# Gate and up products of two feed-forward layers by blocks with seven products in place of eight

## The chip, the cores and the metric

The kernel runs on one core of a Trainium2 chip. Its engines are TensorE (PE in the profile, PEld its weight loads), VectorE (DVE), ScalarE (ACT), GpSimd (POOL) and SyncE (SP, which issues most of the transfers); each works through its own instructions in order and waits for the others by semaphores. The metric is the device time of one execution in microseconds, smaller is better. Before the change it was 1977.13 us, the median of 3 runs (1977.07 to 1987.16).

## The reference

Two transformer blocks follow each other on 512 tokens of width 1024, in float32. Both end with a gated feed-forward layer of width 2816, and only these two layers change:

```python
hffn = modulate(rmsnorm(x, g_norm2[l]), shift2, scale2)
a, u = jnp.split(jnp.einsum('bsd,df->bsf', hffn, w_ffn_in[l]), 2, axis=-1)
x = x + gate2[:, None, :] * jnp.einsum('bsf,fd->bsd', jax.nn.silu(a) * u, w_ffn_out[l])
...
h = rmsnorm_2(x, norm_ffn[l])
x = x + (jax.nn.silu(h @ w_ffn_gate[l]) * (h @ w_ffn_up[l])) @ w_ffn_down[l]
```

The rest (modulation, stick-breaking attention and retention in the first block, sparse attention and gated linear attention in the second) is as before.

## The kernel before

Activations lie transposed: a tile holds 128 channels and all 512 tokens. Every float32 operand is split into a high part in the reduced format float32r (ACT, `split` and `weights`, L150 and L172) and the rest as a low part (DVE, L151 and L173). A product of two such operands is three matmuls, high-high, high-low and low-high (`mm3`, L160 to L162). PSUM has banks under four names: g (3), z (2), r (2) and o (1).

`gemm` (L179) makes 256 output columns: per step it takes four tiles of 128 weight rows, 512 KB, which SP loads into a raw tile (L169), splits them into wh and wl, and runs 24 matmuls of 512 columns into two banks; eight weight tiles are two steps, 48 matmuls. There are three raw, wh and wl tiles each. `gemm_halves` (L213) does the same in two halves of 256 tokens, so that the first half can start when half of its input is normed.

`joint` adds an output projection to the residual and norms the result in halves (`fin2`, `fin4`). `ffn_hidden` then walks over 11 pairs of a gate gemm and an up gemm of 256 columns (the first gate gemm in halves): the gate's bank goes through a sigmoid on ACT and a product on DVE (L869, L870), the up's bank is multiplied in on DVE (L873), and the hidden tile is split at once into two p or q tiles (L150, L151). The output projection over 22 hidden tiles follows.

The order on each engine is written by the framework's scheduler from the order of the program and from what is ready by its own estimate; a tile of a name that has no free buffer waits for one to be released. SBUF holds 32 tiles named p and 36 named q of 2 KB per partition, 12 named t, and the raw, wh and wl tiles of 4 KB.

Of the kernel before, what the change touches and what calls it, by code (L numbers as in the profile page):

```python
# [9 lines left out]
F32 = mybir.dt.float32  # L10
# [57 lines left out]
SLOTS = {"p": 32, "q": 36, "t": 12, "k": 3, "raw": 3, "wh": 3, "wl": 3}  # L68
# [7 lines left out]
N_DIRECT = 2  # L76

# [44 lines left out]
def build(tc, A, dump=None):  # L122
    nc = tc.nc
    with ExitStack() as es:
# [3 lines left out]

        def new(tag, dt=F32):
            return P.tile([128, T], dt, tag=tag, name=tag, bufs=SLOTS[tag])  # L130

# [4 lines left out]
        def wtile(tag, shape, dt):  # L136
            return P.tile(shape, dt, tag=tag, name=tag, bufs=SLOTS[tag])

# [74 lines left out]
        def gemm_halves(w, kt, c0, ncol, X, evac, mid=None, n0=0):  # L213
# [4 lines left out]
            for hf in range(2):  # L218
# [11 lines left out]
                if mid is not None:  # L230
                    mid(hf)

# [535 lines left out]
        def ev_merge(n, ps):  # L768
# [79 lines left out]
        H2 = [pair("p") for _ in range(KD)]  # L848

        def fin2(hf, st):  # L850
            rc = small("rc", 16, bufs=2)
            rstd(st, 0, rc, 0)
            R = psum("r")
            spread(R, rc, 0, 2)
            for k in range(KD):
                norm_mod(x2[k], R[:, 0:256], a2[:, k:k + 1], mod[:, 24 + k:25 + k], H2[k], HS[hf])
# [3 lines left out]
        def ffn_hidden(w_a, ca, w_u, cu, X):  # L860
            hid = []
            for c in range(11):
                act = {}

                def ev_a(n, ps, sl=slice(0, T)):
                    s = new("t")
                    if n not in act:
                        act[n] = new("t")
                    nc.scalar.activation(s[:, sl], ps, AF.Sigmoid)  # L869
                    nc.vector.tensor_mul(act[n][:, sl], ps, s[:, sl])  # L870
# [12 lines left out]
        hid = ffn_hidden(A["w_ffn_in"], 0, A["w_ffn_in"], FF, H2)  # L883


# [526 lines left out]
```

## Time and profile before

| | |
|---|---|
| median of the runs | 1977.13 us |
| the profiled execution | 1982.96 us |
| its span, first to last instruction | 1981.2 us |
| mean granted clock of TensorE | 0.976 |
| PE, DVE, ACT, POOL busy | 96%, 54%, 37%, 16% |
| loads of the first layer's gate and up weights | 851.2 to 1093.7 us |
| loads of the second layer's gate and up weights | 1535.7 to 1813.8 us |

The busy shares are of the span of one profiled execution. A matmul's shown duration includes the time until its results are through, in which the next one already runs; what counts is the distance between starts. A group of instructions shows the busy time, the mean of one and the idle time of its engine just before, with what ended it.

### The profile page before, as it was taken

The page shows a single profiled execution, that of the slowest core. Times are in us where ns is not written, and L with a number is a line of the kernel's source. Part 1 is how long each engine was busy: PE and PEld are TensorE (multiplying, and loading weights), DVE is VectorE, ACT ScalarE, POOL GpSimd, SP SyncE. Part 2 cuts the span into 40 slices and gives each one's busy share as a digit, 9 for nine tenths or more (in the row PEclk, how much of TensorE's full clock was granted, in tenths as well). Part 3 has the DMA queues.
Part 4 walks back from the last instruction along what each step waited for, and adds up shares of the span by engine and source line. Part 5 has one row for each costly group of instructions (what it writes and reads, how often), then busy time and mean ns, then how long its engine had stood idle before and what let it go on. Part 6 is the DMA issues. An engine that isn't in the chain of part 4 may idle for free. (4 is left out here: it accounts for less than half of the span.)

```text
span 1981.2 us, 24637 instructions
## 1 busy us (share of the span) xinstructions
PE 1897.3 (96%) x9561; PEld 1575.5 (80%) x9561; DVE 1074.8 (54%) x1754; ACT 729.4 (37%) x1250; POOL 315.0 (16%) x357
## 2 busy tenths in 40 slices
PE   6889999999999999999999999979999999999998
PEld 4678777888879898888888888767877788888886
DVE  6888876645464554663443322587377653443222
ACT  3466654233322323343222222552255532222222
POOL 3232211102030302010000012232343300000000
PEclk7999999999999999999999999989899999999999
DMA  6612222433424244523332233232133123333222
GB/s 210 203 54 65 65 64 86 159 123 107 133 90 139 77 137 124 195 77 105 96 93 90 89 112 114 79 102 64 31 93 101 49 70 96 96 96 89 92 85 75
DMA packets 193521, 199.25 MB, mean 101 GB/s; under 512 B 9718, under 2 KB 178692, under 8 KB 193404
## 3 DMA queue, kind: packets, MB, share of 16 engines
q1 hardware_dynamic: 189920, 188.48, 30.9%
q0 software_dynamic: 3136, 9.08, 1.4%
q8 instruction: 75, 1.23, 0.3%
q14 instruction: 42, 0.34, 0.1%
q10 hardware_dynamic: 348, 0.13, 0.0%
HBM read 189.25 MB, written 9.99 MB: 101 GB/s over the span
## 5 line engine op out<-in xcount | busy, mean ns | idle before, releaser
L160 PE MATMUL ps_g<-p,wh 128*128 128x512 f32 (+1 forms) x1464 | 579.7, 399 | 8.5 <-DVE q L475 2.6
L161 PE MATMUL ps_g<-p,wh 128*128 128x512 f32 (+1 forms) x1464 | 576.6, 394 | 2.8 <-DVE p L405 2.8
L162 PE MATMUL ps_g<-p,wl 128*128 128x512 f32 (+1 forms) x1464 | 575.9, 394 | 0.0
L173 DVE TENSOR_TENSOR wl<-raw,wh 128x1024 fp32r<-128x1024 f32 (+1 forms) x262 | 325.3, 1242 | 448.9 <-ACT wh L172 448.0
L172 ACT CAST wh<-raw 128x1024 fp32r<-128x1024 f32 (+1 forms) x282 | 294.4, 1044 | 651.7 <-PE ps_g L161 378.9
L160 PEld LDWEIGHTS ps_g<-p,wh 128*128 128x128 f32 x1464 | 276.5, 190 | 74.0 <-issue 7.7
L161 PEld LDWEIGHTS ps_g<-p,wh 128*128 128x128 f32 x1464 | 277.5, 190 | 63.5 <-DVE p L405 3.6
L162 PEld LDWEIGHTS ps_g<-p,wl 128*128 128x128 f32 x1464 | 277.1, 189 | 62.6
L203 PE MATMUL ps_g<-wh,p 128*128 128x256 f32 x512 | 149.1, 292 | 1.5 <-ACT wh L172 1.5
L204 PE MATMUL ps_g<-wl,p 128*128 128x256 f32 x512 | 146.4, 286 | 1.2 <-DVE wl L173 1.2
L205 PE MATMUL ps_g<-wh,p 128*128 128x256 f32 x512 | 146.6, 286 | 0.0
L160 PE MATMUL ps_g<-q,wh 128*128 128x512 f32 (+1 forms) x368 | 142.4, 390 | 0.1
L161 PE MATMUL ps_g<-q,wh 128*128 128x512 f32 (+1 forms) x368 | 142.1, 386 | 0.0
L162 PE MATMUL ps_g<-q,wl 128*128 128x512 f32 (+1 forms) x368 | 142.0, 386 | 0.0
L203 PEld LDWEIGHTS ps_g<-wh,p 128*128 128x128 f32 x512 | 99.6, 195 | 2.8 <-ACT wh L172 1.9
L204 PEld LDWEIGHTS ps_g<-wl,p 128*128 128x128 f32 x512 | 99.8, 195 | 1.9 <-DVE wl L173 1.4
L205 PEld LDWEIGHTS ps_g<-wh,p 128*128 128x128 f32 x512 | 99.7, 195 | 0.0
L160 PEld LDWEIGHTS ps_g<-q,wh 128*128 128x128 f32 x368 | 69.5, 189 | 15.5 <-DVE p L790 0.3
L162 PEld LDWEIGHTS ps_g<-q,wl 128*128 128x128 f32 x368 | 69.5, 189 | 15.0
L161 PEld LDWEIGHTS ps_g<-q,wh 128*128 128x128 f32 x368 | 69.5, 189 | 14.6
L150 ACT CAST q<-t 128x512 fp32r<-128x512 f32 (+1 forms) x68 | 39.1, 581 | 87.2 <-DVE t L873 48.8
L319 DVE SCALAR_TENSOR_TENSOR adaacc<-raw,cact,adaacc 128x256 f32<-128x256 f32 x112 | 53.9, 481 | 27.2 <-DMA raw<-in_w_ada 25.4
(373 smaller groups left out, 2619.4 us busy)
## 6 DMA issues: line engine op xcount, KB each, us to landing
raw<-in_w_in SPq DMA_DIRECT2D x108, 512.0 KB, 3.6
raw<-in_w_ffn_in SPq DMA_DIRECT2D x44, 512.0 KB, 3.5
raw<-in_w_ada SPq DMA_DIRECT2D x32, 512.0 KB, 3.4
raw<-in_w_ffn_gate SPq DMA_DIRECT2D x22, 512.0 KB, 3.6
raw<-in_w_ffn_up SPq DMA_DIRECT2D x22, 512.0 KB
raw<-in_w_ffn_down SPq DMA_DIRECT2D x22, 512.0 KB, 3.7
raw<-in_w_ffn_out SPq DMA_DIRECT2D x19, 512.0 KB, 3.4
raw<-in_w_proj_ret SPq DMA_DIRECT2D x16, 512.0 KB, 3.3
```

What stands on the lines that cost most here:

```text
L150: nc.scalar.copy(hi, src)
L160: nc.tensor.matmul(ps, lh, rh, start=start, stop=False)
L161: nc.tensor.matmul(ps, lh, rl, start=False, stop=False)
L162: nc.tensor.matmul(ps, ll, rh, start=False, stop=stop)
L172: nc.scalar.copy(wh, raw)
L173: low_engine["e"].tensor_tensor(out=wl, in0=raw, in1=f(wh), op=ALU.subtract)
L203: nc.tensor.matmul(o, xh[:, ts], wh[:, i], start=k == 0 and t % 2 == 0, stop=False)
L204: nc.tensor.matmul(o, xh[:, ts], wl[:, i], start=False, stop=False)
L205: nc.tensor.matmul(o, xl[:, ts], wh[:, i], start=False, stop=k == KD - 1 and t % 2 == 1)
L319: nc.vector.scalar_tensor_tensor(out=acc, in0=w, scalar=c, in1=acc, op0=ALU.mult, op1=ALU.add)
```

## The change

For nine of the eleven pairs of a layer, gate and up columns are computed together as a product of two by two blocks. X is cut into halves of tokens (i) and of channels (j), X11 to X22; the weights into halves of channels (i) and into gate (j = 1) and up (j = 2). Seven products, each of 256 tokens, 512 channels and 256 columns (24 matmuls of 256 columns), with weight sums T and activation sums S, take the place of eight:

- 1: X11 with W11; 2: X12 with W21;
- 6: T6 = W11 + W12 + W22; 7: T7 = W12 + W22; 5: T5 = W11 + W12; 3: W22; 4: T4 = W11 + W12 + W21 + W22.

The sums of X are made once per layer (`Normed.sums`) on DVE; signs are chosen so that all weight combinations are sums, and the up results come out negated, which the last product undoes. Products 1, 6, 5 and 3 accumulate in one bank, copied out in between by ACT; 2 has its own; 7 and 4 share a third (`Block.after`).

The weight sums are transfers from SBUF to SBUF that add to their destination, issued by POOL (`Block.add`): raw(1,2) into raw(1,1), which is T5; T5 into a second load of W22 (T6); raw(2,2) into raw(1,2) (T7); T6 into raw(2,1) (T4). A block has five loads of 512 KB, one of them that second load, and four adds of 512 KB. `woven` sets the order 1 2 6 7 5, then 1 of the next block, 3, 4, 2 of the next block, and so on; `play` prepares two products ahead.

The first two pairs of a layer stay plain, in halves (`gemm_quarters`), while the sums of X are formed. All hidden tiles stay whole in 22 p tiles and are split at the end. The memory of q, raw, wh and wl becomes a region that is laid out for the mixing part or for the blocks (16 S tiles of 4 KB, 5 raw) and changes four times; a tile of the new layout waits for the tiles whose memory it takes. The merged activations go to p tiles instead of q.

```diff
 NVEC = _o
-SLOTS = {"p": 32, "q": 36, "t": 12, "k": 3, "raw": 3, "wh": 3, "wl": 3}
+SLOTS = {"p": 32, "t": 12, "k": 3}
+MIX = {"q": 36, "raw": 3, "wh": 3, "wl": 3}
+FFN = {"S": 16, "raw": 5, "wh": 3, "wl": 3}
...
+        region = {}
+        def lay_out(slots):
+            if region:
+                region.pop("es").close()
+            region["es"] = ExitStack()
+            region["pool"] = region["es"].enter_context(tc.tile_pool(name="rg", bufs=1, reuse_waits="tile"))
+            region["slots"] = slots
+        es.callback(lambda: region.pop("es").close())
         def new(tag, dt=F32):
-            return P.tile([128, T], dt, tag=tag, name=tag, bufs=SLOTS[tag])
+            if tag in SLOTS:
+                return P.tile([128, T], dt, tag=tag, name=tag, bufs=SLOTS[tag])
+            return region["pool"].tile([128, T], dt, tag=tag, name=tag, bufs=region["slots"][tag])
...
         def wtile(tag, shape, dt):
-            return P.tile(shape, dt, tag=tag, name=tag, bufs=SLOTS[tag])
+            return region["pool"].tile(shape, dt, tag=tag, name=tag, bufs=region["slots"][tag])
...
+        def gemm_quarters(w, c0, X, evac, n0=0):
+            ws = [weights(w, b, 4, c0, 256) for b in (0, 4)]
+            for hf in range(2):
+                ps = psum("gz"[hf])
+                for n in range(2):
+                    s = slice(n * 128, n * 128 + 128)
+                    for k in range(KD):
+                        wh, wl = ws[k // 4]
+                        xh, xl = X.at(k, hf)
+                        o = ps[:, n * 256:n * 256 + 256]
+                        st, sp = n == 0 and k == 0, n == 1 and k == KD - 1
+                        nc.tensor.matmul(o, wh[:, k % 4, s], xh, start=st, stop=False, skip_group_check=True)
+                        nc.tensor.matmul(o, wh[:, k % 4, s], xl, start=False, stop=False, skip_group_check=True)
+                        nc.tensor.matmul(o, wl[:, k % 4, s], xh, start=False, stop=sp, skip_group_check=True)
+                for n in range(2):
+                    evac(n0 + n, hf, ps[:, n * 256:n * 256 + 256])
+        lay_out(MIX)
...
-            merged[n] = split_new(P2[n], "q")
+            merged[n] = split_new(P2[n], "p")
...
+        lay_out(FFN)
...
-        H2 = [pair("p") for _ in range(KD)]
+        class Normed:
...
+            def quarter(self, i, j):
+                if (i, j) not in self.Q:
+                    self.Q[i, j] = [wtile("S", [128, 4, 256], F32R) for _ in range(2)]
+                return self.Q[i, j]
...
+            def sums(self):
+                def of(i, j, k):
+                    return self.X[4 * (j - 1) + k][:, HS[i - 1]]
+                t = {n: [new("t") for _ in range(2)] for n in (6, 7)}
+                tt = {n: [x.rearrange("p (k n) -> p k n", n=256) for x in t[n]] for n in t}
+                for k in range(4):
+                    a, b, c, d = of(1, 1, k), of(1, 2, k), of(2, 1, k), of(2, 2, k)
+                    s2, s3 = tt[6][k // 2][:, k % 2], tt[7][k // 2][:, k % 2]
+                    nc.vector.tensor_sub(s3, a, c)
+                    nc.vector.tensor_sub(c, d, c)
+                    nc.vector.scalar_tensor_tensor(out=s2, in0=c, scalar=-1.0, in1=a, op0=ALU.mult, op1=ALU.subtract)
+                    nc.vector.scalar_tensor_tensor(out=a, in0=b, scalar=-1.0, in1=s2, op0=ALU.mult, op1=ALU.subtract)
+                    yield
+                for n in (6, 7, 5, 3):
+                    self.S[n] = [wtile("S", [128, 4, 256], F32R) for _ in range(2)]
+                    hi, lo = self.S[n]
+                    if n in t:
+                        for h in range(2):
+                            split(tt[n][h], hi[:, 2 * h:2 * h + 2], lo[:, 2 * h:2 * h + 2])
+                    else:
+                        for k in range(4):
+                            split(of(2 if n == 5 else 1, 1, k), hi[:, k], lo[:, k])
+                    yield
+                self.S[1], self.S[2], self.S[4] = self.Q[1, 1], self.Q[1, 2], self.Q[2, 2]
+                del self.Q[2, 1]
...
+            def add(self, out, a):
+                nc.gpsimd.dma_start(out, a, accum_op=ALU.add)
+            def prep(self, i):
+                raw = self.raw
+                if i == 1:
+                    self.load(1, 1)
+                    src = raw[1, 1]
+                elif i == 2:
+                    self.load(2, 1)
+                    src = raw[2, 1]
+                elif i == 6:
+                    self.load(1, 2)
+                    self.load(2, 2)
+                    t5, t7, t4 = raw[1, 1], raw[1, 2], raw[2, 1]
+                    self.add(t5, raw[1, 2])
+                    t6 = wtile("S", [128, self.kn, 256], F32)
+                    self.load(2, 2, t6)
+                    self.add(t6, t5)
+                    self.add(t7, raw[2, 2])
+                    self.add(t4, t6)
+                    self.T = {6: t6, 7: t7, 5: t5, 3: raw[2, 2], 4: t4}
+                    src = t6
+                else:
+                    src = self.T[i]
+                wh = wtile("wh", [128, self.kn, 256], F32R)
+                wl = wtile("wl", [128, self.kn, 256], F32R)
+                split(src, wh, wl)
+                self.w[i] = wh, wl
+            BANK = {1: "A", 6: "A", 5: "A", 3: "A", 2: "B", 7: "C", 4: "C"}
+            TAG = {"A": "g", "B": "z", "C": "r"}
+            def product(self, i):
+                b = self.BANK[i]
+                first, last = i in (1, 2, 7), i in (3, 2, 4)
+                if first:
+                    self.ps[b] = psum(self.TAG[b])
+                ps = self.ps[b]
+                wh, wl = self.w.pop(i)
+                sh, sl = self.X.S[i]
+                for n in range(2):
+                    o = ps[:, n * 256:n * 256 + 256]
+                    s = slice(n * 128, n * 128 + 128)
+                    for k in range(self.kn):
+                        st = first and n == 0 and k == 0
+                        sp = last and n == 1 and k == self.kn - 1
...
+                            nc.tensor.matmul(o, wh[:, k, s], sh[:, k], start=st, stop=False, skip_group_check=True)
+                            nc.tensor.matmul(o, wh[:, k, s], sl[:, k], start=False, stop=False, skip_group_check=True)
+                            nc.tensor.matmul(o, wl[:, k, s], sh[:, k], start=False, stop=sp, skip_group_check=True)
...
+            def after(self, i):
+                if i in (1, 6, 5):
+                    self.sb[i] = new("t")
+                    nc.scalar.copy(self.sb[i], self.ps["A"])
+                if i == 2:
+                    nc.vector.tensor_add(self.sb[1], self.ps["B"], self.sb[1])
+                    self.out(1, 1, self.sb[1])
+                if i in (5, 7) and {5, 7} <= self.done:
+                    nc.vector.tensor_add(self.sb[5], self.ps["C"], self.sb[5])
+                    self.out(2, 2, self.sb[5])
+                if i == 3:
+                    self.out(1, 2, self.ps["A"])
+                if i == 4:
+                    nc.vector.tensor_add(self.sb[6], self.ps["C"], self.sb[6])
+                    self.out(2, 1, self.sb[6])
+        def play(steps):
+            for b, i in steps[:2]:
+                b.prep(i)
+            for n, (b, i) in enumerate(steps):
+                if n + 2 < len(steps):
+                    c, j = steps[n + 2]
+                    c.prep(j)
+                b.product(i)
+                yield b, i
+        def woven(blocks):
+            steps = []
+            for n, b in enumerate(blocks):
+                if n == 0:
+                    steps += [(b, 1), (b, 2)]
+                steps += [(b, 6), (b, 7), (b, 5)]
+                if n + 1 < len(blocks):
+                    c = blocks[n + 1]
+                    steps += [(c, 1), (b, 3), (b, 4), (c, 2)]
+                else:
+                    steps += [(b, 3), (b, 4)]
+            return steps
...
-        def ffn_hidden(w_a, ca, w_u, cu, X):
...
-                def ev_u(n, ps):
-                    nc.vector.tensor_mul(act[n], ps, act[n])
-                    i = len(hid)
-                    hid.append(split_new(act[n], "p" if i < 4 else "q"))
-                if c == 0:
-                    gemm_halves(w_a, KD, ca, 256, X, lambda n, hf, ps: ev_a(n, ps, HS[hf]))
-                else:
-                    run(gemm(w_a, KD, ca + 256 * c, X, ev_a))
-                run(gemm(w_u, KD, cu + 256 * c, X, ev_u))
-            return hid
+        def ffn_hidden(wa, ca, wu, cu, X):
+            hid = [new("p") for _ in range(2 * N_PLAIN)]
+            sums = X.sums()
+            act = {}
...
+            for c in range(N_PLAIN):
+                gemm_quarters(wa, ca + 256 * c, X, ev_a, n0=2 * c)
+                gemm_quarters(wu, cu + 256 * c, X, ev_u, n0=2 * c)
+                for _ in range(4):
+                    next(sums, None)
+            run(sums)
+            blocks = []
+            for s in range(N_PLAIN, 11):
+                hold = {}
+                hid += [new("p") for _ in range(2)]
+                def out(i, j, c, s=s, hold=hold):
+                    if j == 1:
+                        g = new("t")
+                        nc.scalar.activation(g, c, AF.Sigmoid)
+                        (nc.vector if i == 1 else nc.gpsimd).tensor_tensor(out=c, in0=c, in1=g, op=ALU.mult)
+                    hold[i, j] = c
+                    if (i, 1) in hold and (i, 2) in hold:
+                        for e in range(2):
+                            es = slice(e * 256, e * 256 + 256)
+                            nc.vector.scalar_tensor_tensor(out=hid[2 * s + e][:, HS[i - 1]], in0=hold[i, 2][:, es], scalar=-1.0,
+                                                           in1=hold[i, 1][:, es], op0=ALU.mult, op1=ALU.mult)
+                blocks.append(Block((range(0, 4), range(4, 8)), ((wa, ca + 256 * s), (wu, cu + 256 * s)), X, out))
+            for _ in play(woven(blocks)):
+                pass
+            lay_out(MIX)
+            return [split_new(h, "q" if 2 <= i < 20 else "p") for i, h in enumerate(hid)]
```

## Rows read from the trace of the kernel before

**Rows 1.** The page: span, engines' busy time, granted clock in 40 slices.

```profile
span 1981.2 us, 24637 instructions
...
PE 1897.3 (96%) x9561; PEld 1575.5 (80%) x9561; DVE 1074.8 (54%) x1754; ACT 729.4 (37%) x1250; POOL 315.0 (16%) x357
...
PEclk7999999999999999999999999989899999999999
```

**Rows 2.** Windows: length, busy us by engine, clock, DMA share, GB/s.

```profile
906.00:1096.00 190.00, 190.00 (x816) 153.05 (x816) 74.71 (x84) 54.68 (x68) 0.00 (x0) 1.00 0.31 94
...
1614.00:1819.00 205.00, 205.00 (x880) 165.07 (x879) 80.80 (x91) 58.94 (x73) 0.00 (x0) 1.00 0.33 95
```

**Rows 3.** Timeline of PE, 512 columns (start, us): first and last of 80.

```profile
1085.24 0.40 PE L161 MATMUL ps_g<-p,wh 128*128 128x512 f32 x1
...
1103.68 0.40 PE L162 MATMUL ps_g<-p,wl 128*128 128x512 f32 x1
```

**Rows 4.** Timeline of PE, 256 columns: first and last of 48.

```profile
862.03 0.28 PE L160 MATMUL ps_g<-q,wh 128*128 128x256 f32 x1
...
867.60 0.27 PE L162 MATMUL ps_g<-q,wl 128*128 128x256 f32 x1
```

**Rows 5.** Groups by line, 906 to 1096 us: busy us, mean ns, idle before.

```profile
L173 DVE TENSOR_TENSOR wl<-raw,wh 128x1024 fp32r<-128x1024 f32 x34 | 41.7, 1226 | 86.8 <-ACT wh L172 86.8
L172 ACT CAST wh<-raw 128x1024 fp32r<-128x1024 f32 x34 | 35.8, 1052 | 96.6 <-PE ps_g L161 60.3 <-issue 36.3
...
L873 DVE TENSOR_TENSOR t<-ps_g,t 128x512 f32<-128x512 f32 x16 | 11.1, 691 | 11.6 <-PE ps_g L162 11.6
L869 ACT ACTIVATE t<-ps_g 128x512 f32<-128x512 f32 x18 | 10.7, 594 | 17.4 <-PE ps_g L162 17.4
...
L150 ACT CAST q<-t 128x512 fp32r<-128x512 f32 x14 | 8.6, 617 | 19.0 <-DVE t L873 19.0
```

**Rows 6.** Timeline of DVE, operations on 256 columns.

```profile
875.06 0.48 DVE L399 SCALAR_TENSOR_TENSOR t<-p,a,ps_r 128x256 f32<-128x256 f32 x1
...
893.88 0.42 DVE L870 TENSOR_TENSOR t<-ps_z,t 128x256 f32<-128x256 f32 x1
```

**Rows 7.** Groups by line, engine POOL.

```profile
L799 POOL TENSOR_TENSOR t<-t 128x512 f32<-128x512 f32 x22 | 32.6, 1498 | 116.7 <-ACT t L797 112.7 <-issue 3.6
...
L626 POOL DMA_DIRECT2D m1spill<-t x8 | 4.3, 543 | 41.6 <-DVE t L625 41.6
```

**Rows 8.** DMA issues: queue, count, KB each, median us from issue to landing.

```profile
raw<-in_w_ffn_in SPq DMA_DIRECT2D x44, 512.0 KB, 3.5
...
m1spill<-t POOLq DMA_DIRECT2D x8, 256.0 KB, 3.2
...
gt<-gd POOLq DMA_DIRECT2D x1, 1548.0 KB, 11.3
```

**Rows 9.** Waits of SP's queue: waiter, what it waited for, us, times, longest.

```profile
SPq L169 <- DVE wl L173: 1150.7, 197, 29.5
```

**Rows 10.** Timeline of PE where the gate gemm in halves meets the up gemm.

```profile
886.35 0.28 PE L160 MATMUL ps_z<-p,wh 128*128 128x256 f32 x1
886.47 0.39 PE L161 MATMUL ps_g<-p,wh 128*128 128x512 f32 x1
886.70 0.40 PE L162 MATMUL ps_g<-p,wl 128*128 128x512 f32 x1
886.94 0.28 PE L161 MATMUL ps_z<-p,wh 128*128 128x256 f32 x1
```

**Rows 11.** End of the first stage: window, then SP and DVE in the timeline.

```profile
1096.00:1136.00 40.00, 40.00 (x173) 32.25 (x172) 15.22 (x17) 10.73 (x13) 0.00 (x0) 1.00 0.28 91
...
1099.21 6.01 SPq L169 DMA_DIRECT2D raw<-in_w_ffn_out  x2
...
1122.31 0.69 DVE L873 TENSOR_TENSOR t<-ps_g,t 128x512 f32<-128x512 f32 x1 [0.73 <-PE ps_g L162]
```

More of the change, by code (lines that the diff above doesn't have):

```diff
@@ L76 @@
 N_DIRECT = 2
+N_PLAIN = 2
 class Feed:
@@ new lines, in build, with __init__, load @@
+        class Block:
+            def __init__(self, rows, cols, X, out, tok=False):
+                self.rows, self.cols, self.X, self.out, self.tok = rows, cols, X, out, tok
+                self.kn = len(rows[0])
+                self.raw, self.w, self.ps, self.sb = {}, {}, {}, {}
+                self.done = set()
+            def load(self, i, j, t=None):
+                if t is None:
+                    t = self.raw[i, j] = wtile("raw", [128, self.kn, 256], F32)
+                w, c = self.cols[j - 1]
+                ks, a = self.rows[i - 1], 0
+                while a < len(ks):
+                    b = a + 1
+                    while b < len(ks) and ks[b] == ks[b - 1] + 1:
+                        b += 1
+                    nc.sync.dma_start(t[:, a:b], w[ks[a] * 128:(ks[a] + b - a) * 128, c:c + 256]
+                                      .rearrange("(k p) n -> p k n", p=128))
+                    a = b
+            def add(self, out, a):
[42 more added lines that the diff above has]
+                        sp = last and n == 1 and k == self.kn - 1
+                        if self.tok:
+                            nc.tensor.matmul(o, sh[:, k, s], wh[:, k], start=st, stop=False, skip_group_check=True)
+                            nc.tensor.matmul(o, sh[:, k, s], wl[:, k], start=False, stop=False, skip_group_check=True)
+                            nc.tensor.matmul(o, sl[:, k, s], wh[:, k], start=False, stop=sp, skip_group_check=True)
+                        else:
+                            nc.tensor.matmul(o, wh[:, k, s], sh[:, k], start=st, stop=False, skip_group_check=True)
+                            nc.tensor.matmul(o, wh[:, k, s], sl[:, k], start=False, stop=False, skip_group_check=True)
+                            nc.tensor.matmul(o, wl[:, k, s], sh[:, k], start=False, stop=sp, skip_group_check=True)
+                self.done.add(i)
+                self.after(i)
+            def after(self, i):
[13 more added lines that the diff above has]
+                    self.out(2, 1, self.sb[6])
@@ L850, in fin2 @@
+        X2 = Normed()
         def fin2(hf, st):
@@ L854, in fin2 @@
             spread(R, rc, 0, 2)
-            for k in range(KD):
-                norm_mod(x2[k], R[:, 0:256], a2[:, k:k + 1], mod[:, 24 + k:25 + k], H2[k], HS[hf])
+            X2.put(hf, (lambda k: a2[:, k:k + 1], None, x2), lambda k: mod[:, 24 + k:25 + k], R[:, 0:256])
         joint(A["w_out"], KD, merged, x2, 16, [None], fin2)
         show("x2", x2)
-        def ffn_hidden(w_a, ca, w_u, cu, X):
[L861 to L870, printed above, removed]
-                def ev_u(n, ps):
-                    nc.vector.tensor_mul(act[n], ps, act[n])
-                    i = len(hid)
-                    hid.append(split_new(act[n], "p" if i < 4 else "q"))
-                if c == 0:
-                    gemm_halves(w_a, KD, ca, 256, X, lambda n, hf, ps: ev_a(n, ps, HS[hf]))
-                else:
-                    run(gemm(w_a, KD, ca + 256 * c, X, ev_a))
-                run(gemm(w_u, KD, cu + 256 * c, X, ev_u))
-            return hid
@@ L1315, in build @@
         bg.drain()
+        lay_out(FFN)
         show("cat", [cat[n] for n in range(8)])
-        H4 = [pair("p") for _ in range(KD)]
+        X4 = Normed()
         def fin4(hf, st):
@@ L1324, in fin4 @@
             spread(R, rc, 0, 2)
-            for k in range(KD):
-                norm_mod(x3[k], R[:, 0:256], col("norm_ffn_2", k), None, H4[k], HS[hf])
+            X4.put(hf, (lambda k: col("norm_ffn_2", k), None, x3), None, R[:, 0:256])
         joint(A["w_out_2"], 4, cat, x3, None, [None], fin4)
         show("x4", x3)
-        hid = ffn_hidden(A["w_ffn_gate_2"], 0, A["w_ffn_up_2"], 0, H4)
+        hid = ffn_hidden(A["w_ffn_gate_2"], 0, A["w_ffn_up_2"], 0, X4)
         nf = [new("k"), new("k")]
```

29 lines of the change are left out of this document (28 added, 1 removed).

## The prediction

> **What bounds the kernel now.** I read the first and second parts of the page first: TensorE (PE) is busy for 1897.3 of 1981.2 us, VectorE (DVE) for 54%, ScalarE (ACT) for 37%, and the granted clock is at its full level in nearly every slice [rows 1]. Then the view by windows over the two feed-forward stages: from 906 to 1096 us and from 1614 to 1819 us PE is busy all the time at a clock of 1.00, DVE for about 40%, the DMA engines have a share of 0.31 and 0.33, and POOL does nothing [rows 2]. So what counts in these stages is how often a matmul starts, not how long one is said to last. The timeline of PE gives that: 80 matmuls of 512 columns start between 1085.24 and 1103.68 us, one every 18.44 / 79 = 233.4 ns [rows 3]. The same view where the moving operand has 256 columns: 48 start between 862.03 and 867.60 us, one every 5.57 / 47 = 118.5 ns [rows 4]. Two halves (237.0) cost 1.5% more than one whole, so seven halves-by-halves products in place of eight are a true saving if nothing makes PE wait. That "if" is the prediction.
>
> **The blocks.** One block is 256 gate and 256 up columns. Before: 2 x 48 matmuls of 512 columns, 96 x 233.4 = 22.41 us. After: 7 products of 24 matmuls of 256 columns, 168 x 118.5 = 19.91 us; one product takes p = 2.84 us. That is 2.50 us less for each of 18 blocks: -45.0 us. The two plain column blocks of each stage go from one gemm in halves and three whole ones (96 x 118.5 + 144 x 233.4 = 44.98 us) to four in halves (45.50): +0.5 us each stage, +1.0.
>
> **Engines beside PE.** In a block ACT makes 7 high parts of 1.052 us, 3 copies of a bank (0.617, the 512-wide cast) and 2 sigmoids (0.594): 10.4 us of 19.9. DVE makes 7 low parts of 1.226, three bank sums and one product of 0.69, and four last products on 256 columns at 0.48: 13.3 us [rows 5, 6]. POOL has one 512-wide product of 1.50 us and issues four transfers, at 0.54 us each if they cost what its 256 KB stores cost [rows 7]. None is a bound; cover for DVE is a third of the time. In the plain blocks DVE has 8 low parts (9.8), 12 evacuations of 256 columns (5.0 at 0.42), 16 sums of X (7.7) and the splits of the sums (some 6) plus what is left of the norm, 30 to 38 of 45 us: I cost it at nothing, up to 3 us a stage if the splits come late. The extra ACT pass over X in the first stage (16 x 0.4) lies beside PE in the same way.
>
> **The transfers, the unknown.** No accumulating transfer is in this trace. Nearest rows: the POOL queue's 256 KB stores land 3.2 us after issue, its 1548 KB copy after 11.3; SP's 512 KB loads land after 3.5 [rows 8]. Between the two POOL rows each KB costs (11.3 - 3.2) / 1292 = 6.3 ns, which gives 4.8 us for 512 KB. Bounds: 3.5 (as SP's load), and 8.0 if an add counts as 1024 KB because it also reads what it adds to (3.2 + 768 x 0.0063). I take X = 4.8, nearest to the same queue's rows.
>
> Where it bites: count a block's time from the start of its product 6; then come 7, 5, the next block's 1, then 3, 4, the next block's 2 and its 6 at 7p. Three wh and wl tiles let a split begin when the product three places earlier ends, and it takes 1.05 + 1.23 us and a hand-over, 2.4. With five raw tiles, and the earliest freed taken first, the next block's fourth load goes out when the split of 3 has read its tile, at 2p + 2.4. The separate copy of the last quarter, t6, stands behind that load on SP's queue (0.4), lands in 3.5, is added to (X), split (2.4) and wanted at 7p: 2p + 2.4 + 0.4 + 3.5 + 4.8 + 2.4 + some 0.6 for hand-overs against 7p, that is 14.1 against 14.2 us. POOL issues in order: the add into t6 waits for its load and for the add into t5, and behind it stand the adds into t7 and t4 and the block before's POOL product; product 7 has 2.8 us more, the others longer, so t6 decides. So at X = 4.8 the adds are just covered and cost nothing; each us above costs 1 us a block, 18 in all; below, nothing is gained. SP's waits show that loads here go out when DVE has let a tile go (1150.7 us of waiting in 197 loads) [rows 9], so that a transfer's length counts from there.
>
> Traffic: 512 KB at 94 GB/s and a share of 0.31 (303 GB/s at a full share) is 1.73 us of all engines. Five loads and four adds are 15.6 of 19.9 us; with adds that count twice, 22.5, more than a block took before. So the upper bound is a bound of both kinds.
>
> The Trainium skill bears on the price ("DMA: Bandwidth & Descriptors", Anatomy of one DMA — SWDGE (gpsimd) path): about 2.0 us and the bytes at 436 GB/s on POOL's path, an estimate of 3.2 us for 512 KB and 4.4 with twice the bytes. No row here shows it for an add; by either figure the steady stall stays nothing, as in my sum.
>
> **Start of the blocks.** The 16 S tiles are full until the plain blocks' last reads of the old X21 quarter, which end some 12 matmuls (1.4 us) before the plain part does; t6 of the first block can be loaded only then. 3.5 + 4.8 + 2.4 - 1.4 = 9.3 us against the 5.7 us of products 1 and 2: PE waits 3.6 us, twice: +7.2. Bounds: 0 (7, which needs no t6, put ahead; the timeline shows the order following readiness, where 512-column matmuls of the up gemm stand among the 256-column ones of the gate gemm [rows 10]) and 2 x 6.8 with X = 8.0.
>
> **Seams.** The memory of q, raw, wh and wl is laid out anew four times: before each output projection and after each set of blocks. Before, PE goes through the end of the first stage without a gap (40.00 of 40 us), its next weights asked for at 1099.21, some 25 us before the last hidden tile leaves PSUM after 1122.31 [rows 11]. After, the first raw, wh and wl tiles lie where tiles of the stage before lay, and the hidden splits wait for them too. If they lie on tiles freed last, a seam costs load and split, 3.5 + 2.4 + 0.6 = 6.5 us; if on tiles freed some products earlier, nothing. X1 and X2 are last read six products before the end, the sums 6 and 7 four and three products before it, so most of the memory is free early: I take 1.5 us each, nearer to nothing, +6.0 (bounds 0 and 26). Merged going to p tiles, and the hidden tensors split late, are hidden in the same seams.
>
> **Sum.** -45.0 + 1.0 + 7.2 + 6.0 = -30.8 us. The profiled execution took 1982.96 us, 1.8 around its span, and comes to 1952.2; the median of the runs is 1977.13, 5.8 lower, and the forecast is 1977.1 - 30.8 = 1946 us.
>
> **Rivals.**
> (A) All covered: no stall at the starts and the seams, -44.0: 1933 us. For it, PE's gap-free seams before and the order by readiness; against it, t6's late memory, which is in the code.
> (B) The adds are slower, and it ends on the other side. One mechanism: an add reads two and so counts double, X = 8.0; t6 then comes 3.2 us late in every block, a period of 23.1 us against 22.41 before. 18 x 0.7 = +12.6, + 1.0, starts 13.6, seams 6.0: +33, 2010 us. It decides from X = 4.8 + 30.8 / 18 (and less by 0.2 for the starts), about 6.3 us. For it: the load that the traffic adds up to; against it: an SBUF copy goes nowhere near HBM, and the POOL rows do.
> The Trainium skill speaks for (B): "Collectives: The Full Stack" (The bandwidth ceiling: the fold count and why AG ≠ RS ≠ AR) says that reductions in the DMA engines run at half the rate of copies, because of the second source read. No row here shows it.
> (C) The gain is lost at the seams: four at 6.5 us instead of 1.5, so -30.8 + 20 = -11, 1966 us; with adds 0.5 us late as well, 1975. For it: three layouts share the same addresses; against it: most are freed early.
>
> **How the numbers follow.** The forecast, from 1936 to 1958: 0.45. (A), below 1936: 0.10. (C), and stalls of up to 1.7 us a block, from 1958 to 1987: 0.20, of which 0.07 below 1967. (B), above 1987: 0.25. About 0.5%, or 10 us, is what a measurement of this kernel tells from no change. Faster: 0.45 + 0.10 + 0.07 = 0.62; same 0.13; slower 0.25. The range for 8 in 10 is 1933 to 2003: it leaves out half of (A) and the upper half of (B). The likeliest case's own range is 1936 to 1958.
>
> **What would show it.** PE's matmul count goes from 9561 to about 11,150 (per stage 96 + 21 x 48 = 1104 before, 4 x 96 + 9 x 168 = 1896 after). In the blocks the period from one product 6 to the next is 19.9 us with PE busy throughout; if it is longer, PE's or ACT's idle time ends on a DMA into t6, and the add's time to landing tells (A) from (B): under 5 us right, over 6.3 wrong. A gap of 3 to 4 us ahead of the first product 6 of each stage shows the start, gaps of under 2 us at the four seams the third term. It is wrong if a product of 256 columns has another pace than 118.5 ns, if ACT or DVE rather than a transfer is late in the steady blocks, or if the granted clock falls in a stage where PE waits.

## The result, and the profile after

The change makes the kernel slower. It takes 2041.23 us (median of 4 runs, 2036.75 to 2043.86) against 1981.22 us for the kernel before beside it (4 runs, 1977.07 to 1987.16); the ratio is 1.031, 95% interval 1.029 to 1.033. I had forecast 1946 us and a range of 1933 to 2003.

First the page of the changed kernel, which answers [rows 1].

```profile
span 2035.0 us, 28477 instructions
...
PE 1876.2 (92%) x11145; PEld 1639.0 (81%) x11145; DVE 1179.3 (58%) x1948; ACT 822.0 (40%) x1402; POOL 406.7 (20%) x447
...
PEclk8999999999999999999999899989999898999999
```

PE has 11,145 matmuls, as forecast, and is busy for 21 us less; yet the span is 53.8 us longer. So PE waits, where before it did not. The windows over the blocks of the two stages answer [rows 2] (length, busy us of PE, PEld, DVE, ACT and POOL, clock, DMA share, GB/s):

```profile
945.00:1120.00 175.00, 155.09 (x1216) 150.71 (x1215) 87.93 (x107) 69.25 (x87) 37.03 (x35) 0.97 0.79 193
1690.00:1890.00 200.00, 177.86 (x1385) 173.35 (x1385) 100.41 (x122) 79.22 (x99) 41.80 (x40) 0.96 0.78 187
```

Before, PE had no idle time in such a window; now it lacks 20 of 175 us, and the granted clock is at 0.97. The DMA share has gone from 0.31 to 0.79. The view of DMA issues gives the price of an add (KB each, median us to landing); `raw<-raw` are the adds into T5 and T7, `S<-raw` those into T6, `raw<-S` those into T4. It answers [rows 8]:

```profile
raw<-raw POOLq DMA_DIRECT2D x36, 512.0 KB, 6.2
...
S<-raw POOLq DMA_DIRECT2D x18, 512.0 KB, 4.5
raw<-S POOLq DMA_DIRECT2D x18, 512.0 KB, 4.6
```

Where one block's time goes, the timeline shows, from the start of one product 6 to the next (start, us, engine, line; in brackets how long the engine had been idle, and what ended it). Rows of several engines are put in order of time:

```profile
965.92 1.23 DVE L169 TENSOR_TENSOR wl<-S,wh 128x1024 fp32r<-128x1024 f32 x1 [5.95 <-ACT wh L168]
...
965.94 0.39 PE L1029 MATMUL ps_g<-S,wh 128*128 128x256 f32 x1 [1.01 <-ACT wh L168]
...
967.07 0.68 DVE L1048 TENSOR_TENSOR t<-ps_r,t 128x512 f32<-128x512 f32 x1
...
968.19 1.04 ACT L168 CAST wh<-raw 128x1024 fp32r<-128x1024 f32 x1 [2.30 <-DMA raw<-raw]
969.14 0.63 ACT L1116 ACTIVATE t<-t 128x512 f32<-128x512 f32 x1
...
969.86 1.78 POOL L1117 TENSOR_TENSOR t<-t 128x512 f32<-128x512 f32 x1 [3.72 <-ACT t L1116]
971.67 0.76 DVE L1122 SCALAR_TENSOR_TENSOR p<-t 128x256 f32<-128x256 f32 x2 [1.17 <-POOL t L1117]
...
972.95 1.21 DVE L169 TENSOR_TENSOR wl<-raw,wh 128x1024 fp32r<-128x1024 f32 x1
...
974.19 0.37 SPq L972 DMA_DIRECT2D raw<-in_w_ffn_in  x1
...
977.35 0.37 SPq L972 DMA_DIRECT2D raw<-in_w_ffn_in  x1
...
978.20 0.89 POOL L977 DMA_DIRECT2D raw<-raw  x1 [6.56 <-DMA raw<-in_w_ffn_in]
984.55 0.88 POOL L977 DMA_DIRECT2D S<-raw  x1 [5.46 <-DMA raw<-raw]
985.10 1.22 POOL L977 DMA_DIRECT2D raw<-raw  x1
...
989.23 1.05 ACT L168 CAST wh<-S 128x1024 fp32r<-128x1024 f32 x1 [6.59 <-DMA S<-raw]
...
990.33 0.39 PE L1029 MATMUL ps_g<-S,wh 128*128 128x256 f32 x1 [0.51 <-ACT wh L168]
```

Read it as a chain: 8.25 us after product 6 begins, the split of product 5 has freed a raw tile (DVE, 972.95), and the load of W12 for the next block goes out (974.19); 4.0 us later the add into T5 can be issued (978.20); it lands after 6.3, and only then goes the add into T6 (984.55); that takes 4.7; the cast takes 1.05, and product 6 starts 24.39 us after the last. The rows from 965.92 to 971.67 show why the tile is free so late. The split of 5 stands in DVE's queue behind the last products of the block before (L1122); these wait for POOL's product (L1117), that for ACT's sigmoid (L1116), and the sigmoid for the block's last bank sum (L1048). That sum has had its product 4 since 962.1, but DVE goes through its queue in order, and ahead of the sum stands the split of T6, for which DVE sits idle 5.95 us. On ACT, the cast of T7 stands ahead of the sigmoid and waits for the add into T7; that costs another 1.4 us. So each T6 that comes late makes the next load late, and the chain closes. The same loop stands in the chain of waits that sets the end, here in the second stage (start, us, what):

```profile
1714.09 1.79 POOL t L1117
...
1716.24 0.42 DVE p L1122
1716.66 0.60 DVE t L1040
1717.26 1.14 DVE wl L169
1718.42 3.59 DMA raw<-in_w_ffn_up
...
1722.57 7.08 DMA raw<-raw
...
1729.94 4.45 DMA S<-raw
...
1738.66 1.81 POOL t L1117
```

It closes after 24.57 us: POOL's product, the DVE work behind it, the split that frees the raw tile, then load, T5, T6. Between T6 and POOL's product it names the issue of T4's add, which stands ahead on POOL; what POOL waits for is the sigmoid, as above. Before, the chain was matmuls alone. Over the whole run the nine blocks of a stage take 221.4 and 221.6 us, 24.6 a block with the wait ahead of the first product 6, where they took 22.41 before and 19.91 had been forecast.

### The profile page after: what moved, and what is told of

Its sections match the earlier page's. It is cut to its first block, busy times and chain, and to the rows that moved or that the text cites. A ratio compares the mean times of both kernels' runs of the same rounds, so it can differ in the third digit from the quotient of the medians.

```text
span 2035.0 us, 28477 instructions
## 1 busy us (share of the span) xinstructions
PE 1876.2 (92%) x11145; PEld 1639.0 (81%) x11145; DVE 1179.3 (58%) x1948; ACT 822.0 (40%) x1402; POOL 406.7 (20%) x447
## 5 line engine op out<-in xcount | busy, mean ns | idle before, releaser
L190 ACT CAST wh<-raw 128x1024 fp32r<-128x1024 f32 x210 | 218.6, 1042 | 408.6 <-PE ps_g L179 219.4
L191 DVE TENSOR_TENSOR wl<-raw,wh 128x1024 fp32r<-128x1024 f32 x190 | 234.2, 1234 | 231.8 <-ACT wh L190 230.7
L178 PE MATMUL ps_g<-p,wh 128*128 128x512 f32 (+1 forms) x824 | 331.2, 406 | 20.7 <-ACT wh L190 12.0
L179 PE MATMUL ps_g<-p,wh 128*128 128x512 f32 (+1 forms) x824 | 328.6, 399 | 4.9 <-DVE p L443 2.7
L180 PE MATMUL ps_g<-p,wl 128*128 128x512 f32 (+1 forms) x824 | 327.2, 398 | 0.0
L1029 PE MATMUL ps_g<-S,wh 128*128 128x256 f32 x576 | 171.3, 297 | 40.4 <-ACT wh L168 22.2
L178 PEld LDWEIGHTS ps_g<-p,wh 128*128 128x128 f32 x824 | 158.1, 193 | 57.1 <-ACT wh L190 12.6
L179 PEld LDWEIGHTS ps_g<-p,wh 128*128 128x128 f32 x824 | 159.1, 193 | 37.4 <-DVE p L443 3.4
L169 DVE TENSOR_TENSOR wl<-raw,wh 128x1024 fp32r<-128x1024 f32 (+1 forms) x112 | 132.9, 1188 | 84.9 <-ACT wh L168 84.9
L1031 PE MATMUL ps_g<-S,wl 128*128 128x256 f32 x576 | 169.8, 295 | 11.9 <-DVE wl L169 11.9
L1030 PE MATMUL ps_g<-S,wh 128*128 128x256 f32 x576 | 167.8, 291 | 0.0
L168 ACT CAST wh<-raw 128x1024 fp32r<-128x1024 f32 (+1 forms) x112 | 113.6, 1016 | 107.6 <-PE ps_g L1030 62.8
L1029 PEld LDWEIGHTS ps_g<-S,wh 128*128 128x128 f32 x576 | 115.4, 200 | 46.9 <-ACT wh L168 25.6
L1030 PEld LDWEIGHTS ps_g<-S,wh 128*128 128x128 f32 x576 | 115.4, 200 | 0.0
```

The lines of the kernel that those rows point to most:

```text
L169: nc.vector.tensor_sub(lo, src, f(hi))
L178: nc.tensor.matmul(ps, lh, rh, start=start, stop=False)
L179: nc.tensor.matmul(ps, lh, rl, start=False, stop=False)
L180: nc.tensor.matmul(ps, ll, rh, start=False, stop=stop)
L190: nc.scalar.copy(wh, raw)
L191: low_engine["e"].tensor_tensor(out=wl, in0=raw, in1=f(wh), op=ALU.subtract)
```

## Experiments

The kernel before took 1981.9 us beside the first four kernels, 1978.9 beside the next four, 1982.1 beside the last four. Two theories. **The loop:** the time is that of the chain above, T5 and T6 one behind the other between the last load and product 6. **The traffic:** it is the DMA engines' capacity, wherever in the order the adds stand.

**1. No adds.**

```
-                nc.gpsimd.dma_start(out, a, accum_op=ALU.add)
+                pass
```

> The four adds of each block are left out (products 6, 7, 5 and 4 run on weights that are not summed); loads, splits and products stay. Theory (a loop of waits through the adds: split of 6, last product of the block before, freed raw tile, load 3.9, add into T5 6.3, add into T6 4.6, split of 6, 24.4 us a block): without the adds the loop is some 11 us shorter than the products, a block takes 20.1 to 21.5 us and the kernel about 2041 - 18 x 3.5 = 1978, between 1965 and 1985. Rival (the engines' own order, above all the wait of product 5 for ACT's copy of its bank, 1.6 us a block, and the seams): the block stays above 23 us, the kernel above 2010.

Measured: 1963.35 us, ratio 0.991 (0.988 to 0.994). The stalls are gone, in the window over the blocks:

```profile
945.00:1110.00 165.00, 164.83 (x1374) 164.62 (x1372) 101.23 (x122) 80.88 (x98) 14.33 (x8) 1.00 0.38 117
```

182.3 us for nine blocks, 20.25 a block. In the changed kernel they were 221.4 and 221.6, so the adds cost 78 us, and nearly every other wait of PE in the blocks (for the copies of banks, too) had come from them. The run is also a bound of this way of working: with the sums for nothing 18 us are won, not the 45 put down for the products.

**2. The same transfers as plain copies.**

```
-                nc.gpsimd.dma_start(out, a, accum_op=ALU.add)
+                nc.gpsimd.dma_start(out, a)
```

> The four transfers of a block copy in place of adding (sums are left out), from the same queue, with the same sizes and waits. If an add is dear because it reads two (rival B of the prediction): a copy lands in 4 to 5 us instead of 6.2 and 4.6, the loop is some 2 to 3 us shorter, the kernel about 1990 to 2005. If the price is that of any 512 KB transfer of this queue beside the loads: landing times stay within 0.5 us and the kernel within 10 us of 2041.

Measured: 1977.0 us, ratio 0.999 (0.996 to 1.001); 188.2 and 190.9 us for nine blocks. With the same order, queue and bytes written, 64 us of the time hang on the word "add" alone, more than the 36 to 51 I had expected:

```profile
945.00:1110.00 165.00, 164.06 (x1362) 163.65 (x1362) 96.39 (x119) 78.59 (x96) 29.45 (x40) 1.00 0.64 222
...
raw<-raw POOLq DMA_DIRECT2D x36, 512.0 KB, 4.1
...
S<-raw POOLq DMA_DIRECT2D x18, 512.0 KB, 3.4
raw<-S POOLq DMA_DIRECT2D x18, 512.0 KB, 2.9
```

An add lands 1.1 to 2.1 us later than a copy. But the traffic falls with it, so this run does not tell the theories apart.

**3. The sigmoid's product on DVE,** which takes POOL's instruction out of the loop.

```
-    (nc.vector if i == 1 else nc.gpsimd).tensor_tensor(out=c, in0=c, in1=g, op=ALU.mult)
+    nc.vector.tensor_tensor(out=c, in0=c, in1=g, op=ALU.mult)
```

> The multiply of sigmoid and gate of the second token half goes from POOL (1.8 us and two hand-overs) to DVE (0.69). Theory (it stands in the loop: DVE's last products wait for it, and the split that frees the raw tile stands behind them): the loop is 1.3 to 2 us shorter, and ACT's copy ahead of product 5 comes earlier, 18 x 1.3 to 2 = 23 to 36 us less, the kernel between 2005 and 2018. Rival (the DMA engines are full, share 0.78): no change, 2036 to 2044.

Measured: 2027.7 us, ratio 1.024 (1.020 to 1.028), 13.5 us less, between the two expectations. The blocks take 219.5 and 217.4 us, only 0.3 us a block less; 4.3 us come from the end of the first stage, where the gap is 3.2 us in place of 7.5. The product is one link; without it the bank sum still stands behind the split of T6 on DVE, and T5's load goes out only 0.6 us earlier: 6.8 us after product 6 in place of 7.4, by the median of 12 blocks each.

**4. No blocks at all,** the layout of memory and the gemms in quarters kept.

```
-N_PLAIN = 2
+N_PLAIN = 11
...
-            sums = X.sums()
+            sums = iter(())
...
-            run(sums)
```

> All eleven pairs of each layer run plain, in halves; regions, hidden tiles split at the end and seams stay; no blocks, no sums, no adds. Prices the seams: against the kernel before, 96 more matmuls pairs of halves per pair cost 3.6 us a layer (7 in all); if the seams cost what the trace of the changed kernel shows (about 10 at the end of the first layer, 3 to 5 at the other ends) the kernel takes 1995 to 2005; if the prediction's 1.5 us a seam held, 1990 or less.

Measured: 2006.2 us, ratio 1.013 (1.009 to 1.017). That is 24 us more than before, but not all of it stands around the blocks: 18 pairs run in halves here that are blocks in the changed kernel, at 192 x 0.120 = 23.04 us in place of 22.41, which is 11 us. Some 13 us are left for what stands around. The stages take 258.9 and 257.8 us: 2112 matmuls at 120.0 ns are 253.4, and the rest falls mostly to the beginning, while the first tiles are normed; the seam behind the first stage is a gap of 5.6 us.

**5 to 8. Who forms which sum.** POOL's own additions in place of transfers: all four, with T6 written as T5 plus the last quarter (5 and 6); T5 and T6 alone (7); T7 and T4 alone (8). Runs 7 and 8 take away the same number of adds.

```
+            def padd(self, out, a):
+                nc.gpsimd.tensor_tensor(out=out, in0=out, in1=a, op=ALU.add)
...
-                    self.add(t5, raw[1, 2])
+                    self.padd(t5, raw[1, 2])
...
-                    self.add(t6, t5)
+                    self.padd(t6, t5)
```

(this is 7; in 8 the two lines are those of t7 and t4; in 5 and 6 all four, without the second load, and 5 has the product on DVE, 6 on POOL)

> All four sums of weights are made by POOL's own additions instead of accumulating transfers; T6 is written as T5 plus the last quarter, so its separate second load goes too; the sigmoid's product is on DVE. Loop theory: the additions take about 2.4 us each (two of the 512-wide rate) where the transfers took 6.2 and 4.6, the chain load, T5, T6, split, DVE falls from 24.4 to some 18 us, PE becomes the bound at 20.3 us a block as without any sums (182 us for nine), and with the seams that stayed in that run the time is 1955 to 1975. Rival, POOL as the next bound: 4 x 2.4 us one after the other and T4 last, in a loop that waits for DVE's splits, or POOL's work making DVE's longer: 22 us a block or more, 1990 to 2010.

> As the run with POOL's additions, but the sigmoid's product stays on POOL, in line with the additions. Loop theory: the product is due while T5 waits for its load, so it costs POOL 1.8 us in a stretch where it is idle: within 5 us of the other run. Rival: POOL is the bound then (4 x 2.4 + 1.8 = 11.5 us of work, in order), and each block is 1 us longer: 18 us more than the other run.

> Only the sums of T5 and T6, the two that stand one behind the other between the last load and product 6, are made by POOL's additions; T7 and T4 stay accumulating transfers, and T6 keeps its own second load, so that half of the accumulating traffic is left. Loop theory: the chain loses 3.9 + 2.2 us of 24.4, and the blocks go to 20.3 to 21 us, 1965 to 1985. Rival, the DMA engines are the bound and not the order: this run and the one with T7 and T4 on POOL save the same traffic and come out alike, some 2000.

> Only the sums of T7 and T4, which are not in the chain that leads to product 6, are made by POOL's additions; T5 and T6 stay accumulating transfers. Loop theory: the chain keeps its two transfers, each at most 1 us shorter with less traffic beside it, so the blocks stay at 22.5 to 24.5 us, 2005 to 2040. Rival, the DMA engines are the bound: the same traffic is saved as with T5 and T6 on POOL, and the two times are alike.

Measured: (7) 1977.8 us, ratio 0.999 (0.997 to 1.001); (8) 2049.6 us, ratio 1.037 (1.034 to 1.040). Windows over the blocks, and a block in the timeline, first of 7:

```profile
945.00:1110.00 165.00, 161.34 (x1336) 160.30 (x1334) 115.18 (x118) 75.56 (x94) 74.20 (x40) 1.00 0.63 169
...
968.72 2.40 POOL L980 TENSOR_TENSOR raw<-raw 128x1024 f32<-128x1024 f32 x1 [6.50 <-DMA raw<-in_w_ffn_in]
971.20 3.27 POOL L980 TENSOR_TENSOR S<-S,raw 128x1024 f32<-128x1024 f32 x1
...
988.93 2.40 POOL L980 TENSOR_TENSOR raw<-raw 128x1024 f32<-128x1024 f32 x1 [6.47 <-DMA raw<-in_w_ffn_in]
```

and then of 8:

```profile
945.00:1120.00 175.00, 155.19 (x1219) 151.73 (x1219) 96.47 (x108) 68.45 (x85) 57.60 (x35) 0.97 0.58 151
...
977.04 0.89 POOL L977 DMA_DIRECT2D raw<-raw  x1 [6.62 <-DMA raw<-in_w_ffn_in]
982.99 0.87 POOL L977 DMA_DIRECT2D S<-raw  x1 [5.06 <-DMA raw<-raw]
...
988.29 2.36 POOL L980 TENSOR_TENSOR raw<-raw,S 128x1024 f32<-128x1024 f32 x1 [2.01 <-DMA S<-raw]
...
989.25 2.48 DVE L169 TENSOR_TENSOR wl<-S,wh 128x1024 fp32r<-128x1024 f32 x1 [5.61 <-ACT wh L168]
...
1001.52 0.89 POOL L977 DMA_DIRECT2D raw<-raw  x1 [6.90 <-DMA raw<-in_w_ffn_in]
```

This settles which of the two comes first. The DMA share falls in both, from 0.79 to 0.63 and 0.58, but from one product 6 to the next it is 20.2 us in the block shown of 7 and 24.5 in that of 8 (20.8 and 24.5 by the mean of both stages), and the times lie 72 us apart. It counts which two adds go, not how many. In 8 the T5 add still takes 6.0 us at a share of 0.58: that is its own price and not a crowd. That 8 is even 8 us slower than the changed kernel I had not expected. A candidate is in the trace: T6's low part, split beside POOL's addition, takes 2.48 us there in place of 1.23, and it stands in the loop; it was not tried by itself. The bank sum stands behind it there, too; at 1.25 us a block that is worth 22 us in 18 blocks (an estimate from these lines), enough to hide what the lighter traffic gives back, but not the 72 us between 7 and 8.

(5) 1964.7 us, ratio 0.992 (0.990 to 0.994), as the loop theory had it; nine blocks take 185.4 us, 3 more than without sums. (6) 1978.0 us, ratio 1.000 (0.998 to 1.001): 13 us more than 5, where I had expected 5 at most or 18. Each stage's blocks take 4.4 us longer, and the seam is 7.5 us again in place of 3.2: in sum 13, by one trace of each.

**9. A sixth raw tile,** the adds left as transfers (and ten temporaries in place of twelve, for the room; 9c is that alone).

```
-SLOTS = {"p": 32, "t": 12, "k": 3}
+SLOTS = {"p": 32, "t": 10, "k": 3}
...
-FFN = {"S": 16, "raw": 5, "wh": 3, "wl": 3}
+FFN = {"S": 16, "raw": 6, "wh": 3, "wl": 3}
```

> The changed kernel with six tiles for raw weights in the blocks in place of five (and ten temporaries in place of twelve, to make room); all adds stay accumulating transfers. Loop theory: the load that T5 waits for takes a tile that was let go one split earlier, 3.0 to 3.2 us by the starts of the loads in the trace (971.18, 974.19, 977.35), so the loop is 21.2 to 21.6 us and the time falls by some 54, to 1980 to 2000, with the adds no shorter than before. Rival, the price of the adds on the DMA engines decides wherever the loads start: less than 15 us are gained, 2025 or more.

> Only the ten temporaries in place of twelve, with five raw tiles: what the room for the sixth tile costs by itself. Loop theory: the temporaries are not in the loop, within 10 us of the changed kernel, 2031 to 2051. Rival: sigmoids and copies wait for one another, 2055 or more.

Measured: 2020.2 us, ratio 1.020 (1.017 to 1.022); 9c 2047.4, ratio 1.032 (1.029 to 1.036). So the earlier load is worth 27 us, half of what I had expected.

```profile
945.00:1120.00 175.00, 160.08 (x1285) 156.81 (x1285) 92.43 (x112) 73.05 (x91) 39.40 (x38) 0.99 0.83 201
```

The block is 23.3 us now, and an add into T5 or T7 lands after 6.4 us. The DMA share is 0.83, which is 19.3 us of all engines a block, near the 20.2 that PE needs: the traffic theory was not empty, but it is the second bound. How much of the missing half is that, I did not separate.

**10 and 11. Best versions,** both from run 5: one plain column block in place of two (10); the first two weight tiles of the projection split ahead of the hidden tensors in the program (11).

```
-N_PLAIN = 2
+N_PLAIN = 1
```

```
...
             lay_out(MIX)
+            ahead.extend([fresh(*a) for a in pre])
             return [split_new(h, "q" if 2 <= i < 20 else "p") for i, h in enumerate(hid)]
...
```

> POOL's additions and the product on DVE as in the best run so far, with one plain column block a stage in place of two, so ten blocks. If the sums of X are still ready in time: each stage trades 192 products at 120.0 ns (23.0 us) for a block of 20.45, twice -2.6: 1957 to 1962. Rival: the sums and their splits, some 14 us of DVE beside the norm, do not fit into one column block and product 6 waits: each us late costs 2 in all, and from 2.6 us a stage it is slower than two plain blocks, 1967 to 1985.

> POOL's additions and the product on DVE; besides, the first two weight tiles of the projection behind the blocks are split ahead of the hidden tensors in the order of the program. The seam at the end of the first stage was 3.2 us there, the first cast of the projection's weights standing behind four casts of hidden tensors on ScalarE (2.4 us). If that order is its cause: the gap falls to about 1 us, 1962 to 1965. Rival: the memory laid out anew is its cause, and it stays at 3 us or more, 1965.

Measured: (10) 1983.2 us, ratio 1.000 (0.999 to 1.002). The rival was right: PE waits for a first product 6, as its timeline shows, 7.1 us in each stage, behind the splits of the sums of X.

```profile
921.69 0.58 PE L1028 MATMUL ps_g<-S,wh 128*128 128x256 f32 x1 [6.81 <-ACT wh L168]
```

(11) 1961.2 us, ratio 0.990 (0.988 to 0.991), the best kernel of the study, 1% faster than before. Its step failed, though: the seam is still 3.2 us, and against run 5 (other runs, 0.992) nothing is shown. ACT casts a hidden tile (`q<-p`) ahead of the weights as before:

```profile
1118.56 0.60 ACT L168 CAST q<-p 128x512 fp32r<-128x512 f32 x1
1119.07 1.04 ACT L197 CAST wh<-raw 128x1024 fp32r<-128x1024 f32 x1
...
1120.16 0.50 PE L178 MATMUL ps_g<-p,wh 128*128 128x512 f32 x1 [2.90 <-ACT wh L197]
```

So the place in the program did not move the cast in ACT's queue, and my edit did not try what it was to try: whether order or memory makes the seam stays open.

## Why the prediction was wrong

The forecast misses by 95 us, and the blocks make 77 of them: -45.0 and +7.2 for the starts was forecast, -37.8 in all; they came to 443.0 us against 403.4, +39.6.

**The failed step** is the sentence "product 7 has 2.8 us more, the others longer, so t6 decides", with which T5's add left the sum. T6 is T5 plus the last quarter, and T5 waits for a load of its own. So between load and product 6 there stand two adds, 6.3 and 4.7 us, and not one. With T5's add struck out, 24.4 - 6.3 = 18.1 us would have stayed under PE's 20.2, and the stall would have been nothing, as forecast; in run 7, which shortens both adds to 2.4 and 3.3, 20.8 us stay. I had written down the dependence ("the add into t6 waits for its load and for the add into t5") and then priced the first half of it.

A second step failed with it: when that load goes out. The prediction let a split begin when the product three places earlier ends, and take 2.4 us; the split of 5 would then free the tile for T5's load 2.4 us after product 6. In run 1, without adds, the load goes at 3.2; in the changed kernel it goes at 8.25 (7.4 by the median of 12 blocks), because the orders of DVE and ACT, which the rule leaves out, put it behind the T6 of the block before. That 8.25 looks like the prediction's 2p + 2.4 = 8.1 is chance: 8.1 was for the fourth load, W22, which goes at 8.2 in run 1 and at 11.4 here (977.35). Neither step alone would have made the stall: with the load at 3.2, two adds in a row would have ended after some 24.4 - 5.0 = 19.4 us (an estimate from the block shown), under the 20.2, too.

**The size of X.** For T5 it was 6.2, near the 6.3 from which I had let rival (B) decide. The rival's sign came true, and in part its mechanism: an add costs more because it is an add (run 2). But (B) put 8.0 us into T6 alone, and its 2010 us were too little, as no rival had the two adds in a row. The Trainium skill's rule for (B) ("Collectives: The Full Stack", The bandwidth ceiling: the fold count and why AG ≠ RS ≠ AR: reductions in the DMA engines at half the rate of copies, for the second source read) is borne out in kind. By an estimate from DMA share times block: 0.79 x 24.6 = 19.4 us with four adds, 0.38 x 20.25 = 7.7 with none, 0.64 x 20.9 = 13.4 with four copies; an add occupies the engines for 2.9 us, a copy for 1.4, twice as long. In time to landing it is 1.3 to 1.6 times. The estimate of 3.2 to 4.4 us by the Trainium skill ("DMA: Bandwidth & Descriptors", Anatomy of one DMA — SWDGE (gpsimd) path) was too low for T5 and near for T6.

**The pace.** I took 118.5 ns a matmul from 48 of another gemm [rows 4]. In the new products, quarters and blocks alike, they start every 120.0 ns, over 1,400 in a row in run 1, while that other gemm keeps its 118.4 in the changed kernel. What in the form of the products makes the 1.3% was not tried. It is 0.25 us a block: -40.5 instead of -45.0 us for the blocks.

**Plain blocks.** +1.0 was forecast. The stretches take 52.3 and 50.5 us, 12.8 above the 2 x 44.98 reckoned for before. About half of that was there before: by its trace the two stages take 248.9 and 250.6 us (876.02 to 1124.91 and 1594.39 to 1845.01), which leaves 47.2 and 48.9 beside nine pairs at 22.41, since the norm's small matmuls stand among the products, too. The change itself costs 6.7. After it, 384 matmuls at 120.0 are 46.1 of each stretch; PE is idle for 2.3 and 0.8 us, and the rest goes to the norm's small matmuls and, from 886.5 to 889.0, to products 0.21 us apart while the granted clock is 0.50. Gemms of the up weights that ran between those of the gate weights [rows 10] are no longer there to fill the gaps; that is argued, not tested.

**Starts.** Right in kind and place: gaps of 5.1 and 3.6 us before the first product 6, where 3.6 each was said. In the first, T6's load took 6.0 us (930.44 to 936.45) for the 3.5 reckoned, the add 4.5 for 4.8. T6's load, add and split end it:

```profile
936.45 0.86 POOL L977 DMA_DIRECT2D S<-raw  x1 [6.72 <-DMA S<-in_w_ffn_in]
...
940.91 1.04 ACT L168 CAST wh<-S 128x1024 fp32r<-128x1024 f32 x1 [5.95 <-DMA S<-raw]
...
942.01 0.58 PE L1029 MATMUL ps_g<-S,wh 128*128 128x256 f32 x1 [4.79 <-ACT wh L168]
```

The matmul behind the gap takes 0.58 us in place of 0.28; from 942.0 to 943.2 us the granted clock is 0.50, the lower of its two levels, and from 930 to 936 it was 1.00; in the two stages 79 and 96 matmuls start 0.15 to 0.32 us after the one before, in place of 0.12.

**Seams.** +6.0 was forecast. The one behind the first stage costs 7.5 us, the one behind the second 2.1; it answers [rows 11], where no gap was:

```profile
1138.55 15.06 SPq L187 DMA_DIRECT2D raw<-in_w_ffn_out  x3
...
1158.85 1.04 ACT L190 CAST wh<-raw 128x1024 fp32r<-128x1024 f32 x1
...
1159.94 0.80 PE L178 MATMUL ps_g<-p,wh 128*128 128x512 f32 x1 [7.20 <-ACT wh L190]
```

The first load is asked for 21 us ahead, so the gap is not load and split, as I had put it (6.5 us): the cast stands in ACT's queue behind those of hidden tiles, and the last of these behind POOL's product. With that product on DVE the gap is 3.2 us (runs 3, 5, 10 and 11), with it on POOL 7.5 (runs 1, 2 and 6 to 9). The two stretches behind the stages, which the change does not touch but for memory, got 2.4 and 2.5 us shorter. The first of them takes from 465.4 to 474.2 us in the thirteen kernels here that have the new layout, so nothing can be read from that.

## What to carry to other kernels

When an operation of unknown price enters a chain, write down the whole chain from the event that starts it to the one that waits, with every dependence in it, and add up all the links before judging which ones "decide"; a sum of a sum is two links. Go on to what frees the buffer that the chain starts with: an engine that works in order brings in everything that stands ahead in its queue, here the split of T6, ahead of a bank sum that had been ready for 5 us. When a resource and an order are both suspects, take the same load off twice, once in the chain and once beside it (runs 7 and 8): equal times mean the resource, unequal ones the order. Take an engine's pace from the form of instruction that the change will run; 1% of it was 4.5 us here.

## What the runs showed of the hardware that was not expected

An accumulating transfer of 512 KB within SBUF lands after 4.5 to 6.2 us, where the same transfer as a copy takes 2.9 to 4.1. POOL's own addition of the same 128 x 1024 values takes 2.40 us alone, less than either (20 subtractions of that size on POOL in the kernel before took 2.43 on average, so this price could have been read in advance), but 3.4 beside DVE's splits, and these suffer as well. By-line groups of DVE and POOL in run 5, over its blocks:

```profile
L169 DVE TENSOR_TENSOR wl<-raw,wh 128x1024 fp32r<-128x1024 f32 x49 | 90.2, 1840 | 21.7 <-ACT wh L168 21.7
...
L977 POOL TENSOR_TENSOR raw<-raw,S 128x1024 f32<-128x1024 f32 x8 | 27.2, 3395 | 0.0
L169 DVE TENSOR_TENSOR wl<-S,wh 128x1024 fp32r<-128x1024 f32 x8 | 22.1, 2760 | 0.0
```

The same split took 1226 ns before [rows 5]. The Trainium skill ("SBUF — State Buffer", Who interferes with whom) says that only the port pair that DVE and GpSimd share makes engines wait for one another, and that it goes to one of them for a whole instruction; the trace agrees, with instructions of both engines drawn out by 0.6 to 1.5 us, and with one pair in run 8: POOL's addition, begun first at 988.29, takes its usual 2.36 us, while DVE's split, begun at 989.25, takes 2.48 and ends 1.1 us after it. PE hides that here: it loses 3 us in nine blocks.
